# The turned S5 scan: where the swapped operand is written, and where copies, lengths, samples and Toeplitz loads stand

## The chip, the core and the metric

The kernel runs on one core of a Trainium2 chip. The metric is the device time of one execution in microseconds, the median of several runs. TensorE (PE in the profile) does the matrix products, VectorE (DVE), ScalarE (ACT) and GpSimd (POOL) work on tiles, and transfers are issued from the queues of SyncE (SP) and of GpSimd.

## The reference, cut to what matters

The reference is one step of a two-layer decoder: layer 0 mixes tokens with an HGRN2 gated recurrence, layer 1 with an S5 complex diagonal recurrence; each layer has a SwiGLU channel mixer and a per-layer embedding ("ple"). There are 512 prompt tokens and 8 samples of 8 tokens, D = 1024. The change lies in the S5 mixer of layer 1:

```
bu = einsum('btgc,gpc->btgp', u, b_bar);  bu[:, 0] += lam_bar * h0
h  = associative_scan(s5_combine, (lam_bar, bu))       # h_t = lam_bar * h_(t-1) + bu_t, complex
y  = einsum('btgp,gcp->btgc', h, c_mat).real + d * u;  y = gelu(y)
val, gate = split(y @ w_glu);  out = val * sigmoid(gate);  new states: h[:, -1]
```

It has 64 groups of 16 channels with 64 complex states each. The samples start from h0, the prompt from zero.

## The kernel before

**Accuracy.** Products are taken in three parts (`mm3`, L299 to L301): the weight and the activation are each split into a high and a low part (whi, wlo; xh, xl), and whi·xh, whi·xl and wlo·xh are added in one PSUM bank. A weight tile is loaded to `wraw`, copied by ScalarE to `whi` (L200, `copy`), and subtracted on another engine to `wlo` (L203, `tt`); in the S5 stage that engine is GpSimd, and GpSimd's queue issues the loads of `wraw` (L226). There are four PSUM banks named `mm`.

**Chunks.** S5 is computed in chunks of 8 tokens, 36 to a block, in two blocks of 288 columns. Block 0 holds the first KA = 28 chunks of the prompt and the 8 samples (one chunk each), block 1 the prompt's other 36. `z_part(blk, o, ...)` multiplies octet o (8 groups) of the tokens `u` by the input matrices `zw` (L1447). ScalarE copies the result out of PSUM: the chunks' inputs go to `HS[blk]` (tiles "xl", 128 x 64 x 36; partitions 0 to 63 real, 64 to 127 imaginary), the last ones to `ZL`.

**The turned scan.** The recurrence over chunks is complex. The kernel turns every input backward by a rotation that depends on group and chunk, scans with real factors, and turns the result forward. The rotation tables are `C` (name "turn") and `Z` (name "xh"), which are loaded from `tb_scratch` (L1577). A quarter is 16 groups. In `turn`, two multiplies of 64 partitions each make the cross term with halves exchanged (into `pr`, L203), a third multiplies by C, and a fourth adds or subtracts. `run_on` does the scan (L1533) with the factors `rho` spread over 35 columns, and then `lengths` copies the next quarter's factors into the single buffer (L1529). All of this is on VectorE.

**The order in `layer0_to_1`.** It runs under a manual schedule: each engine's instructions stand in the order in which the program writes them, and an engine works through them strictly in that order.

1. While the ple of layer 0 ends (`tails`, `pj` and `xf` rows at L203 and L206), the queue of SP issues two octets of the Toeplitz matrices `mg` (L1453), then the two tables.
2. For block 0, octet by octet, `z_part(0, o)`, with the ple tail of block 1 in between (`start(1, ...)`, `settle(1)`). Then VectorE scans the four quarters of block 0.
3. SP stores the layer's result (`u_scratch`) and loads it as `u` in 16 pieces. TensorE computes the projection of layer 1's embedding (`ple_proj`), which ScalarE copies to `pj1`.
4. GpSimd's queue loads the samples' state h0 into a tile `sm` (L1618). ScalarE scales it into HS[0] in place of the samples' columns, behind the block-0 scan (L197). Then `z_part(1, o)`.
5. `lag_part` (Toeplitz products within a chunk) and `out_part` (products of the states, added to u by VectorE, gelu by ScalarE, stored to `y_scratch`, loaded back by `y_load`), with the block-1 scan (`last_states`) on VectorE in steps between them.
6. `last_samples` advances the samples by their last chunk, on GpSimd (SE = 1) at the first lag, scales on ScalarE and stores (L1632, `out_s5s`).
7. `y_load` splits the loaded y into XH (ScalarE) and XL; for block 0 all eight XL splits are on GpSimd. XL[0] uses the memory of HS[0] once that is no longer read. Then come the GLU products, four banks at first, and the sigmoid (`gs`).

Of the kernel before, what the change touches and what calls it, by code (L numbers as in the profile page):

```python
# [8 lines left out]
FP32 = mybir.dt.float32  # L9
# [3 lines left out]
ACT = mybir.ActivationFunctionType  # L13
OP = mybir.AluOpType
# [18 lines left out]
KA = 28  # L33
# [32 lines left out]
SCAN_AT = ((2, 4, 10, 16, 20, 26, 30, 34, 38, 42, 46, 50, 54, 60, 68, 74), (2, 4, 6, 9, 12, 15, 17, 19, 21, 23, 26, 33, 34, 36, 41, 45))  # L66
QWAIT = 9
SIDE = 1
OCT = 2
TB = 3  # L70
SL = (0, 0, 1, 0, 1, 0, 1, 0)
SO0 = (0, 1, 0, 1, 0, 1, 0, 1)
SE = 1
SO = 0
SF = 3
YD = 4
WX = 3
AB = 2
# [64 lines left out]
def hybrid_decoder_kernel(ctx: ExitStack, tc: tile.TileContext, a: dict):  # L143
    nc = tc.nc
# [37 lines left out]
    SGN, NSG = sgn[:, 0:1], sgn[:, 1:2]  # L182
# [13 lines left out]
    def act(out, in_, func, bias=None, scale=1.0):  # L196
        nc.scalar.activation(out, in_, func, bias=ZERO if bias is None else bias, scale=scale)  # L197

    def copy(out, in_):
        nc.scalar.activation(out, in_, ACT.Copy)  # L200

    def tt(out, x, y, op, eng=None):
        (eng or nc.vector).tensor_tensor(out, x, y, op=op)  # L203
# [137 lines left out]
    def settle(blk):  # L341

        while any(it[1] == blk for it in later):
            it = next(it for it in later if it[1] == blk)
            later.remove(it)
            it[2]()
        if blk in tails:
            run(tails.pop(blk))
# [10 lines left out]
    def step(g, n=1):  # L359
        for _ in range(n):  # L360
            if next(g, StopIteration) is StopIteration:
                return False
        return True
# [11 lines left out]
    class LayerNorm:  # L375
# [747 lines left out]
    mg_d = nc.dram_tensor("mg_scratch", (128, NG, 128), FP32).ap()  # L1123
# [287 lines left out]
    U, HS = {}, {}  # L1411
# [11 lines left out]
    def step_rows(scratch):  # L1423
        return scratch.rearrange("s c g k -> (s c) (g k)")
# [10 lines left out]
    def u_load(m, blk):  # L1435
        nc.sync.dma_start(U[blk][:, 8 * m:8 * m + 8, :].rearrange("p g k -> p (g k)"), step_rows(u_d[blk, m]))

    def products(w, o, x):

        ps = mm_bank()
        xo = x[:, 8 * o:8 * o + 8, :].rearrange("p g k -> p (g k)")
        for j in range(8):
            c = slice(36 * j, min(36 * j + SW, NB))
            for r in (0, 64):
                nc.tensor.matmul(ps[r:r + 64, c], w[:, j, r:r + 64], xo[:, c], start=True, stop=True)  # L1447
                passed(0.2)
        return ps[:, :NB].rearrange("p (g k) -> p g k", k=36)

    def octet(pool, src, o, tag, bufs, eng=None):
        t = pool.tile([128, 8, 128], FP32, tag=tag, name=tag, bufs=bufs)
        (eng or nc.sync).dma_start(t, src[:, 8 * o:8 * o + 8, :])  # L1453
        return t

    def z_part(blk, o, zw):

        v = products(zw, o, U[blk])
        g = slice(8 * o, 8 * o + 8)
# [38 lines left out]
    def chunk_state(j):  # L1498
        return HS[0][:, :, j] if j < KA else HS[1][:, :, j - KA]

    def advance(out, hj, z, n=None, work=None, lam=lam8, gs=slice(0, NG), eng=None):

        ng = gs.stop - gs.start

        def b(t):
            return t[:, gs] if n is None else t[:, gs, None].to_broadcast([128, ng, n])
        sh = [128, NG] if n is None else [128, NG, n]
        m, c = work or [const.tile(sh, FP32, tag=t, name=t, bufs=AB) for t in ("am", "ac")]
        lrb, lib = b(lam[:, 0]), b(lam[:, 1])
        tt(m, hj, lrb, OP.mult, eng)  # L1510
        tt(c[0:64], hj[64:128], lib[64:128], OP.mult, eng)
        tt(c[64:128], hj[0:64], lib[0:64], OP.mult, eng)
        tt(m, m, z, OP.add, eng)
        tt(out, m, c, OP.add, eng)

    def turn(blk, q, back):

        gs, n = slice(16 * q, 16 * q + 16), slice(1, 36 if blk else KA + 1)  # L1520
        h, c, C, Z = (x[:, n] if len(x.shape) == 2 else x[:, :, n] for x in
                      (HS[blk][:, gs], s5["c"], s5["C"][:, gs], s5["Z"][:, gs]))
        tt(c[0:64], h[64:128], Z[64:128], OP.mult)
        tt(c[64:128], h[0:64], Z[0:64], OP.mult)
        tt(h, h, C, OP.mult)
        tt(h, h, c, OP.add if back else OP.subtract)

    def lengths(q):
        nc.vector.tensor_copy(s5["rho"][:, :, 1:36], rho[:, 16 * q:16 * q + 16, None].to_broadcast([128, 16, 35]))  # L1529

    def run_on(blk, q):
        h = HS[blk][:, 16 * q:16 * q + 16].rearrange("p g k -> p (g k)")
        nc.vector.tensor_tensor_scan(h, s5["rho"].rearrange("p g k -> p (g k)"), h, 0.0, op0=OP.mult, op1=OP.add)  # L1533
        lengths((q + 1) % 4)

    s5 = {}

    def layer0_to_1():
# [28 lines left out]
        st.update(lo=nc.gpsimd, split=SPLIT_S5, limit=N_SLOTS)  # L1567
        op_pool = ExitStack()
        op = op_pool.enter_context(tc.tile_pool(name="op", bufs=1, side="right"))
        mg, cl = [octet(op, mg_d, o, "mg", OCT) for o in range(OCT)], []  # L1570

        s5["C"] = op.tile([128, NG, 36], FP32, name="turn")
        turn_z = {}
# [1 line left out]
        s5["Z"] = turn_z[1]  # L1575
        for n, x in enumerate((s5["C"], s5["Z"])):
            nc.sync.dma_start(x.rearrange("p g k -> p (g k)"), tb_d[:, n].rearrange("p g k -> p (g k)"))  # L1577
        s5["rho"], s5["c"] = (x for x in s5["zp"].tile([128, 2, 16, 36], FP32, tag="praw", name="pr2").rearrange(
            "p n g k -> n p g k"))
        settle(0)  # L1580
        for b in range(2):
            chunk_tiles("xl", HS, b)
        nc.vector.memset(HS[0][:, :, 0:1], 0.0)
        nc.vector.memset(s5["rho"][:, :, 0:1], 0.0)
        lengths(0)


        for o in range(8):
            z_part(0, o, s5["zw"][o])
            if o == 1:  # L1590
                start(1, LIGHT)
            elif o > 1:
                step(tails[1], 2)
        settle(1)
        for q in range(4):
            turn(0, q, True)
            run_on(0, q)
            turn(0, q, False)
        nc.vector.tensor_copy(HS[1][:, :, 0], HS[0][:, :, KA])
        left.close()  # L1600
        pj1 = left.enter_context(tc.tile_pool(name="pp1", bufs=1)).tile([128, KD, T], FP32, name="pj1")
# [3 lines left out]
        for b in (1, 0):  # L1605
            U[b] = U["both"][:, b]
            for n in range(KD):
                u_load(n, b)


        def samples(tag, n=1):
            t = s5["zp"].tile([128, n, NG, 8], FP32, tag=tag, name="sm")
            return [t[:, i] for i in range(n)]
# [2 lines left out]
        run(proj)  # L1616
        h0, = samples("phi")
        nc.gpsimd.dma_start(h0, a["h0"])  # L1618
        act(HS[0][:, :, KA:36], h0, ACT.Identity, scale=NSG)
        for o in range(8):  # L1620
            z_part(1, o, s5["zw"][o])
            if len(mg) < 8:
# [3 lines left out]
        so, tmp = samples("plo", 2)  # L1626

        def last_samples():
            advance(so, HS[0][:, :, KA:36], ZL[:, :, 0:8], 8, (so, tmp), eng=SE and nc.gpsimd)
            yield  # L1630
            act(so, so, ACT.Identity, scale=NSG)
            nc.gpsimd.dma_start(a["s5s"], so)  # L1632
            yield

        samples_end = last_samples()
# [3 lines left out]
        def last_states():  # L1639
            for q in range(4):  # L1640
                turn(1, q, True)
                run_on(1, q)
                yield
                turn(1, q, False)
                yield
            advance(po, chunk_state(63), ZL[:, :, 8])
            nc.vector.tensor_scalar(po, po, NSG, None, op0=OP.mult)
            nc.gpsimd.dma_start(a["s5o"], po)
            yield
# [5 lines left out]
        def y_start(b, o):  # L1655

            if o > 1:
                y_loads[b, o - 2] = y_load(b, o - 2, yt[b][o - 2])
                step(y_loads[b, o - 2])

        yt = [[U[0][:, 8 * o:8 * o + 8].rearrange("p g k -> p (g k)") for o in range(8)]] * 2
        for o in range(8):
            lag_part(o, mg[o])
            if o >= OCT:
                cl.append(octet(s5["zq"], cl_d, len(cl), "zw", 8))
            step(scan, SL[o])
            if o == SO:
                step(samples_end)
        for o in range(8):
            out_part(0, o, cl[o])  # L1670
            y_start(0, o)
            step(scan, SO0[o])
            if o >= YD:
                step(y_loads[0, o - YD])
            if o == SF:
                step(samples_end)
        y_start(0, 8)
        y_start(0, 9)
        for o in range(8 - YD, 8):
# [8 lines left out]
        with more_weights(WX, (p0 + 128) // 8):  # L1688
            for blk, m in [(b, m) for h in (0, 4) for b in range(2) for m in range(h, h + 4)]:
                p = p0 + 16 * m  # L1690
# [205 lines left out]
```

## Time and profile before

| | |
|---|---|
| median of 3 runs | 1588.85 us (1588.47 to 1592.74) |
| the profiled execution | 1589.6 us |
| its span | 1587.8 us |
| mean granted TensorE clock | 0.983 |
| busy: PE, DVE, ACT, POOL | 95%, 60%, 43%, 22% of the span |
| the S5 stage with the change | about 896 to 994 us |

Times in the views are microseconds from the start of the span. A row of a timeline gives start, duration, engine, line, operation, output and inputs with their shapes, and in brackets the idle time ahead of it and what ended that. A row of the waits gives who waited for what: total, number, longest. A row of the groups gives the count, the busy time and mean nanoseconds of one, and the idle time before.

### The profile page before, as it was taken

Reading aid. Unit: us, or ns where it says so; the run is one execution under the profiler, and the core shown is the slowest. Engines: PE = TensorE matmul, PEld = TensorE weight load, DVE = VectorE, ACT = ScalarE, POOL = GpSimd, SP = SyncE. Lnnn points to the kernel's source line nnn. Section 1 sums busy time; section 2 is a strip of 40 time slices with the busy share of each in tenths; the row PEclk is TensorE's granted clock in tenths of the full one; section 3 lists DMA queues with packets and bytes.
Section 4 is the critical chain, followed back from the end, with each engine's and each line's share of the span. In section 5 each row is a group of like instructions: output and inputs, shape, how many; then the busy total and the mean of one; then the engine's idle time right before and its main releaser. Section 6 shows DMA issues by size and latency. Waiting matters only on the chain. (4 is left out here: it accounts for less than half of the span.)

```text
span 1587.8 us, 30040 instructions
## 1 busy us (share of the span) xinstructions
PE 1514.9 (95%) x12550; PEld 1467.1 (92%) x12550; DVE 947.1 (60%) x1711; ACT 687.9 (43%) x1152; POOL 342.9 (22%) x447
## 2 busy tenths in 40 slices
PE   8899999899999999999999947999999999999998
PEld 7898989788999999999989947899999999999997
DVE  4848484868547778953486699457433233334685
ACT  5546464746532223123278524436432222123375
POOL 1303030302003768860022332302000000000111
PEclk9999999999999999999999978999999999999999
DMA  5223131232224877663214986432222222223121
GB/s 185 95 69 101 63 109 64 100 115 80 68 70 145 216 185 216 195 182 108 98 54 170 233 209 179 101 107 80 67 80 93 80 81 93 81 80 120 31 78 60
DMA packets 97255, 180.32 MB, mean 114 GB/s; under 512 B 41888, under 2 KB 56912, under 8 KB 96864
## 3 DMA queue, kind: packets, MB, share of 16 engines
q1 hardware_dynamic: 88144, 151.92, 31.3%
q0 software_dynamic: 8976, 26.49, 6.2%
q8 instruction: 98, 1.61, 0.4%
q14 instruction: 37, 0.30, 0.1%
HBM read 151.08 MB, written 27.30 MB: 112 GB/s over the span
## 5 line engine op out<-in xcount | busy, mean ns | idle before, releaser
L299 PE MATMUL mm<-xh,whi 128*128 128x288 f32 x2048 | 609.7, 298 | 9.5 <-ACT xh L200 6.5
L300 PE MATMUL mm<-xl,whi 128*128 128x288 f32 x2048 | 608.9, 297 | 5.0 <-POOL xl L203 3.5
L301 PE MATMUL mm<-xh,wlo 128*128 128x288 f32 x2048 | 606.6, 296 | 1.3 <-DVE wlo L203 1.3
L299 PEld LDWEIGHTS mm<-xh,whi 128*128 128x128 f32 x2048 | 387.8, 189 | 15.9 <-ACT xh L200 7.6
L300 PEld LDWEIGHTS mm<-xl,whi 128*128 128x128 f32 x2048 | 387.9, 189 | 8.4 <-POOL xl L203 5.0
L301 PEld LDWEIGHTS mm<-xh,wlo 128*128 128x128 f32 x2048 | 387.8, 189 | 1.5 <-DVE wlo L203 1.5
L200 ACT ACTIVATE whi<-wraw 128x1024 fp32r<-128x1024 f32 x208 | 218.7, 1053 | 250.1 <-DMA wraw<-in_w_dram 117.2
L203 DVE TENSOR_TENSOR wlo<-wraw,whi 128x1024 fp32r<-128x1024 f32 x200 | 247.1, 1252 | 33.2 <-ACT whi L200 32.8
L299 PE MATMUL mm<-hhi,whi 128*128 128x288 f32 x704 | 209.3, 297 | 0.0
L301 PE MATMUL mm<-hhi,wlo 128*128 128x288 f32 x704 | 207.5, 295 | 0.0
L300 PE MATMUL mm<-hlo,whi 128*128 128x288 f32 x704 | 207.2, 294 | 0.0
L203 DVE TENSOR_TENSOR fs<-fs,mm 128x288 f32<-128x288 f32 x88 | 39.9, 454 | 254.5 <-PE mm L301 241.4
L203 POOL TENSOR_TENSOR ln_s<-ln_s,xf 128x288 f32<-128x288 f32 x24 | 24.3, 1012 | 570.9 <-DVE xf L203 451.2
L299 PEld LDWEIGHTS mm<-hhi,whi 128*128 128x128 f32 x704 | 132.1, 188 | 1.7 <-issue 1.4
L300 PEld LDWEIGHTS mm<-hlo,whi 128*128 128x128 f32 x704 | 132.1, 188 | 0.3
L301 PEld LDWEIGHTS mm<-hhi,wlo 128*128 128x128 f32 x704 | 132.0, 188 | 0.0
L299 PE MATMUL mm<-xhi,whi 128*128 128x320 f32 (+1 forms) x384 | 121.5, 316 | 0.0
L300 PE MATMUL mm<-xlo,whi 128*128 128x320 f32 (+1 forms) x384 | 113.3, 295 | 0.0
L301 PE MATMUL mm<-xhi,wlo 128*128 128x320 f32 (+1 forms) x384 | 113.2, 295 | 0.0
L200 ACT ACTIVATE hhi<-fs 128x288 fp32r<-128x288 f32 x88 | 38.8, 441 | 152.1 <-DVE fs L203 152.1
L197 ACT ACTIVATE fs<-mm,eps 128x288 f32<-128x288 f32 x88 | 44.1, 502 | 131.0 <-PE mm L301 130.9
L299 PEld LDWEIGHTS mm<-xhi,whi 128*128 128x128 f32 x384 | 72.7, 189 | 6.9 <-issue 4.4
(318 smaller groups left out, 2273.9 us busy)
## 6 DMA issues: line engine op xcount, KB each, us to landing
wraw<-in_w_dram SPq DMA_DIRECT2D x198, 512.0 KB
wraw<-in_w_dram POOLq DMA_DIRECT2D x10, 512.0 KB, 7.1
S<-in_s_dram SPq DMA_DIRECT2D x8, 512.0 KB
out_hgs_dram<-So SPq DMA_DIRECT2D x8, 512.0 KB
wr<-wt_scratch SPq DMA_DIRECT2D x16, 256.0 KB
bT<-in_s5bt_dram SPq DMA_DIRECT2D x16, 256.0 KB
cl_scratch<-cl POOLq DMA_DIRECT2D x16, 256.0 KB, 6.1
zw_scratch<-zw POOLq DMA_DIRECT2D x16, 256.0 KB, 6.5
```

The lines of the kernel that those rows point to most:

```text
L197: nc.scalar.activation(out, in_, func, bias=ZERO if bias is None else bias, scale=scale)
L200: nc.scalar.activation(out, in_, ACT.Copy)
L203: (eng or nc.vector).tensor_tensor(out, x, y, op=op)
L299: nc.tensor.matmul(out, whi, rhi, start=start, stop=False)
L300: nc.tensor.matmul(out, whi, rlo, start=False, stop=False)
L301: nc.tensor.matmul(out, wlo, rhi, start=False, stop=stop)
```

## The change

1. `z_part(0, o)`: ScalarE writes each octet's prompt inputs twice more, half by half with the halves exchanged, into a tile `swap` (one for a quarter, two buffers). The backward turn of block 0 then multiplies that tile by Z in one instruction of 128 partitions, in place of two of 64, and subtracts in place of adding.
2. `lengths` goes from VectorE to GpSimd and has two buffers: two copies at the start, and six more, each of which waits for a scan.
3. Quarter 0 of block 0 is scanned inside the loop over `z_part(0, o)`, ahead of block 1's ple tail; quarters 1 to 3 follow that tail.
4. The loads of `mg` are issued after the 16 loads of u, not before the tables; one goes to a tile of its own (OCT = 1), seven to used `zw` tiles.
5. h0 is scaled on VectorE.
6. The samples' advance is on VectorE, after the whole block-1 scan.

The core of the diff:

```diff
-OCT = 2
+OCT = 1
...
         if blk == 0:
             copy(HS[0][:, g, 1:36], v[:, :, 0:35])
+            q, i = divmod(o, 2)
+            if i == 0:
+                swapped[q] = s5["op"].tile([128, 16, 36], FP32, tag="swap", name="swap", bufs=2)
+            x = swapped[q][:, 8 * i:8 * i + 8, 1:KA + 1]
+            copy(x[0:64], v[64:128, :, 0:KA])
+            copy(x[64:128], v[0:64, :, 0:KA])
             copy(ZL[:, g, 0:8], v[:, :, KA:36])
...
-        tt(c[0:64], h[64:128], Z[64:128], OP.mult)
-        tt(c[64:128], h[0:64], Z[0:64], OP.mult)
+        if back and not blk:
+            tt(c, c, Z, OP.mult)
+        else:
+            tt(c[0:64], h[64:128], Z[64:128], OP.mult)
+            tt(c[64:128], h[0:64], Z[0:64], OP.mult)
         tt(h, h, C, OP.mult)
-        tt(h, h, c, OP.add if back else OP.subtract)
+        tt(h, h, c, OP.add if back and blk else OP.subtract)
...
-        nc.vector.tensor_copy(s5["rho"][:, :, 1:36], rho[:, 16 * q:16 * q + 16, None].to_broadcast([128, 16, 35]))
+        nc.gpsimd.tensor_copy(s5["rho"][q % 2][:, :, 1:36],
+                              rho[:, 16 * q:16 * q + 16, None].to_broadcast([128, 16, 35]))
...
-        lengths((q + 1) % 4)
+        if (blk, q) < (1, 2):
+            lengths((q + 2) % 4)
+
+    def scan_quarter(blk, q):
+        turn(blk, q, True)
+        run_on(blk, q)
+        turn(blk, q, False)
...
-        mg, cl = [octet(op, mg_d, o, "mg", OCT) for o in range(OCT)], []
...
             if o == 1:
                 start(1, LIGHT)
+                scan_quarter(0, 0)
             elif o > 1:
                 step(tails[1], 2)
         settle(1)
-        for q in range(4):
-            turn(0, q, True)
-            run_on(0, q)
-            turn(0, q, False)
+        for q in range(1, 4):
+            scan_quarter(0, q)
...
                 u_load(n, b)
+        mg, cl = [octet(op, mg_d, o, "mg", OCT) for o in range(OCT)], []
...
-        act(HS[0][:, :, KA:36], h0, ACT.Identity, scale=NSG)
+        nc.vector.tensor_scalar(HS[0][:, :, KA:36], h0, NSG, None, op0=OP.mult)
...
-            advance(so, HS[0][:, :, KA:36], ZL[:, :, 0:8], 8, (so, tmp), eng=SE and nc.gpsimd)
+            advance(so, HS[0][:, :, KA:36], ZL[:, :, 0:8], 8, (so, tmp))
...
+            step(samples_end, 2)
             advance(po, chunk_state(63), ZL[:, :, 8])
...
             step(scan, SL[o])
-            if o == SO:
-                step(samples_end)
```

In the changed file the lines up to about 1450 stand three lower (L203 becomes L200, L200 becomes L197, L226 becomes L223); L1529 becomes L1539, L1533 L1544, L1618 L1637.

On GpSimd, from block 1's `xf` additions to the load of h0 (`sm`), before:

```order
L203 TENSOR_TENSOR xf<-xf,pj 128x288 [waits DVE_49] x4
L203 TENSOR_TENSOR wlo<-wraw,whi 128x1024 [waits DMASW1_49,PE_49,Activation_49]
L226 DMA wraw<-in_w_dram 128x1024 [waits DMASW3_49,Pool_49]
L203 TENSOR_TENSOR wlo<-wraw,whi 128x1024 [waits DMASW2_49,PE_49,Activation_49]
L226 DMA wraw<-in_w_dram 128x1024 [waits DMASW4_49,Pool_49]
L1618 DMA sm<-in_h_dram 128x512 [waits DMASW5_49,PE_49]
```

and after:

```order
L1539 COPY pr_10102<-rho 128x16x35 [waits DVE_49]
L200 TENSOR_TENSOR xf<-xf,pj 128x288 [waits DVE_49] x4
L200 TENSOR_TENSOR wlo<-wraw,whi 128x1024 [waits DMASW1_49,PE_49,Activation_49]
L223 DMA wraw<-in_w_dram 128x1024 [waits DMASW3_49,Pool_49]
L1539 COPY pr_10102<-rho 128x16x35 [waits DVE_49] x3
L200 TENSOR_TENSOR wlo<-wraw,whi 128x1024 [waits DMASW2_49,PE_49,Activation_49]
L223 DMA wraw<-in_w_dram 128x1024 [waits DMASW4_49,Pool_49]
L1637 DMA sm<-in_h_dram 128x512 [waits DMASW5_49,PE_49]
```

Four copies of the lengths stand among these rows now (`pr`; each waits for a scan on VectorE: the first for block 0's quarter 0, the others for its quarters 1, 2 and 3), and the load of h0 stands behind all four.

On VectorE, the end of the block-1 scan (`xl1` is HS[1], `xl0` HS[0], `am` and `ac` the prompt's last state), before:

```order
L1533 SCALAR_TENSOR_TENSOR xl1_10108<-pr2_10106,xl1_10108 128x576 [waits DVE_49]
L1529 COPY pr2_10106<-rho_87 128x16x35 [waits DVE_49]
L203 TENSOR_TENSOR pr2_10106<-xl1_10108,xh1_10103 64x16x35 x2
L203 TENSOR_TENSOR xl1_10108<-xl1_10108,turn_10102 128x16x35 [waits DVE_49]
L203 TENSOR_TENSOR xl1_10108<-xl1_10108,pr2_10106 128x16x35 [waits DVE_49]
L203 TENSOR_TENSOR am_11097<-xl1_10108,lam8_86 128x64 [waits DVE_49]
```

and after:

```order
L1544 SCALAR_TENSOR_TENSOR xl1_10104<-pr2_10102,xl1_10104 128x576 [waits DVE_49,Pool_49]
L200 TENSOR_TENSOR swap_11088<-xl1_10104,xh1_10099 64x16x35 [waits DVE_49]
L200 TENSOR_TENSOR swap_11088<-xl1_10104,xh1_10099 64x16x35
L200 TENSOR_TENSOR xl1_10104<-xl1_10104,turn_10098 128x16x35 [waits DVE_49]
L200 TENSOR_TENSOR xl1_10104<-xl1_10104,swap_11088 128x16x35 [waits DVE_49]
L200 TENSOR_TENSOR sm_10703<-xl0_10103,lam8_86 128x512
L200 TENSOR_TENSOR sm_10703<-xl0_10103,lam8_86 64x512 x2
L200 TENSOR_TENSOR sm_10703<-sm_10703,zl_88 128x512 [waits DVE_49]
L200 TENSOR_TENSOR sm_10703<-sm_10703 128x512 [waits DVE_49]
```

The scan (SCALAR_TENSOR_TENSOR in these rows) now waits for GpSimd, the copy of the lengths is gone from here, and the samples' advance (`sm`) stands behind the last quarter; its first three instructions are the last that read HS[0].

On ScalarE, the copies out of PSUM for octets 4 to 6 of block 0, after:

```order
L197 ACTIVATE xl0_10103<-mm_10242 128x8x35 [waits PE_49]
L197 ACTIVATE swap_10263<-mm_10242 64x8x28 [waits DVE_49]
L197 ACTIVATE swap_10263<-mm_10242 64x8x28
L197 ACTIVATE zl_88<-mm_10242 128x8x8
L197 ACTIVATE xl0_10103<-mm_10267 128x8x35 [waits PE_49]
L197 ACTIVATE swap_10263<-mm_10267 64x8x28 x2
L197 ACTIVATE zl_88<-mm_10267 128x8x8
L197 ACTIVATE xl0_10103<-mm_10288 128x8x35 [waits PE_49]
L197 ACTIVATE swap_10309<-mm_10288 64x8x28 [waits DVE_49,Activation_49]
```

and the same octets before:

```order
L200 ACTIVATE xl0_10107<-mm_10225 128x8x35 [waits PE_49]
L200 ACTIVATE zl_88<-mm_10225 128x8x8
L200 ACTIVATE xl0_10107<-mm_10247 128x8x35 [waits PE_49]
L200 ACTIVATE zl_88<-mm_10247 128x8x8
L200 ACTIVATE xl0_10107<-mm_10266 128x8x35 [waits PE_49]
L200 ACTIVATE zl_88<-mm_10266 128x8x8
```

Two instructions to an octet are added; the first one that writes a reused `swap` tile waits for VectorE.

More of the change, by code (lines that the diff above doesn't have):

```diff
@@ L72 @@
 SO0 = (0, 1, 0, 1, 0, 1, 0, 1)
-SE = 1
-SO = 0
-SF = 3
 YD = 4
@@ L1514, in advance @@
         tt(out, m, c, OP.add, eng)
+    swapped = {}
     def turn(blk, q, back):
         gs, n = slice(16 * q, 16 * q + 16), slice(1, 36 if blk else KA + 1)
-        h, c, C, Z = (x[:, n] if len(x.shape) == 2 else x[:, :, n] for x in
-                      (HS[blk][:, gs], s5["c"], s5["C"][:, gs], s5["Z"][:, gs]))
-        tt(c[0:64], h[64:128], Z[64:128], OP.mult)
-        tt(c[64:128], h[0:64], Z[0:64], OP.mult)
+        if blk and back:
+            swapped[q] = s5["op"].tile([128, 16, 36], FP32, tag="swap", name="swap", bufs=2)
+        h, c, C, Z = (t[:, :, n] for t in (HS[blk][:, gs], swapped[q], s5["C"][:, gs], s5["Z"][:, gs]))
+        if back and not blk:
[3 more added lines that the diff above has]
+            tt(c[64:128], h[0:64], Z[0:64], OP.mult)
         tt(h, h, C, OP.mult)
-        tt(h, h, c, OP.add if back else OP.subtract)
+        tt(h, h, c, OP.add if back and blk else OP.subtract)
     def lengths(q):
-        nc.vector.tensor_copy(s5["rho"][:, :, 1:36], rho[:, 16 * q:16 * q + 16, None].to_broadcast([128, 16, 35]))
+        nc.gpsimd.tensor_copy(s5["rho"][q % 2][:, :, 1:36],
+                              rho[:, 16 * q:16 * q + 16, None].to_broadcast([128, 16, 35]))
     def run_on(blk, q):
         h = HS[blk][:, 16 * q:16 * q + 16].rearrange("p g k -> p (g k)")
-        nc.vector.tensor_tensor_scan(h, s5["rho"].rearrange("p g k -> p (g k)"), h, 0.0, op0=OP.mult, op1=OP.add)
-        lengths((q + 1) % 4)
+        nc.vector.tensor_tensor_scan(h, s5["rho"][q % 2].rearrange("p g k -> p (g k)"), h, 0.0,
+                                     op0=OP.mult, op1=OP.add)
+        if (blk, q) < (1, 2):
[4 more added lines that the diff above has]
+        turn(blk, q, False)
     s5 = {}
@@ L1569, in layer0_to_1 @@
         op = op_pool.enter_context(tc.tile_pool(name="op", bufs=1, side="right"))
-        mg, cl = [octet(op, mg_d, o, "mg", OCT) for o in range(OCT)], []
+        s5["op"] = op
         s5["C"] = op.tile([128, NG, 36], FP32, name="turn")
@@ L1577, in layer0_to_1 @@
             nc.sync.dma_start(x.rearrange("p g k -> p (g k)"), tb_d[:, n].rearrange("p g k -> p (g k)"))
-        s5["rho"], s5["c"] = (x for x in s5["zp"].tile([128, 2, 16, 36], FP32, tag="praw", name="pr2").rearrange(
-            "p n g k -> n p g k"))
+        s5["rho"] = [x for x in s5["zp"].tile([128, 2, 16, 36], FP32, tag="praw", name="pr2").rearrange(
+            "p n g k -> n p g k")]
         settle(0)
@@ L1583, in layer0_to_1 @@
         nc.vector.memset(HS[0][:, :, 0:1], 0.0)
-        nc.vector.memset(s5["rho"][:, :, 0:1], 0.0)
-        lengths(0)
+        for q in range(2):
+            nc.gpsimd.memset(s5["rho"][q][:, :, 0:1], 0.0)
+            lengths(q)
         for o in range(8):
@@ L1674, in layer0_to_1 @@
                 step(y_loads[0, o - YD])
-            if o == SF:
-                step(samples_end)
         y_start(0, 8)
```

## The prediction

> **What bounds the kernel now.** I read the page's busy shares first, then the waits between 896 and 996 us, then the timelines of ScalarE, TensorE, VectorE (DVE) and GpSimd (POOL) there. Before that stretch the change touches nothing; what it is worth is how much earlier or later TensorE gets its work inside it.
>
> ```profile
> PE 1514.9 (95%) x12550; PEld 1467.1 (92%) x12550; DVE 947.1 (60%) x1711; ACT 687.9 (43%) x1152; POOL 342.9 (22%) x447
> ```
>
> TensorE is idle for 73 of 1587.8 us. The two longest waits of the S5 stage:
>
> ```profile
> PE mm L1447 <- ACT zl L200: 12.1, 1, 12.1
> ...
> PE mm L1447 <- DMA u<-u_scratch: 8.2, 1, 8.2
> ```
>
> ScalarE's and TensorE's rows say who holds whom:
>
> ```profile
> 908.30 1.32 ACT L200 ACTIVATE pj<-mm 128x288 f32<-128x288 f32 x4 [3.75 <-POOL xf L203]
> ...
> 918.97 0.69 ACT L200 ACTIVATE pj<-mm 128x288 f32<-128x288 f32 x2
> 943.53 0.81 ACT L197 ACTIVATE xl<-sm,eps,sgn 128x512 f32<-128x512 f32 x1 [23.87 <-DVE xl L1599]
> ...
> 990.45 2.01 ACT L200 ACTIVATE whi<-wraw 128x1024 fp32r<-128x1024 f32 x2 [3.11 <-DVE xl L203]
> ```
>
> ```profile
> 926.75 5.94 PE L1447 MATMUL mm<-u,zw 128*64 128x64 f32 x128 [8.19 <-DMA u<-u_scratch]
> ...
> 979.11 0.61 PE L299 MATMUL mm<-xh,whi 128*128 128x288 f32 x1 [1.43 <-DVE u L203]
> ...
> 992.50 0.29 PE L301 MATMUL mm<-xh,wlo 128*128 128x288 f32 x1
> ...
> 994.32 0.40 PE L299 MATMUL mm<-xh,whi 128*128 128x288 f32 x1 [1.52 <-ACT gs L197]
> ```
>
> ScalarE's scaling of h0 at 943.53 stands behind DVE's whole block-0 scan, and TensorE behind ScalarE. Then DVE's block-1 scan runs; the first GLU units start at 979.11, last until 992.79 (13.7 us), and TensorE goes on at 994.32, 3.87 us after ScalarE's whi copies began at 990.45. So DVE bounds the stage, and 979.11 and 994.32 are the marks that matter: from there TensorE has work, and a shift of the second mark goes to the end.
>
> **The change, step by step.** All times are on the clock of before. DVE's rows of block 0:
>
> ```profile
> 900.45 0.52 DVE L206 SCALAR_TENSOR_TENSOR pj<-pj,vec,pr 128x288 f32<-128x288 f32 x1 [4.36 <-ACT pr L197]
> ...
> 909.65 2.08 DVE L203 TENSOR_TENSOR pr<-xl,xh 64x448 f32<-64x448 f32 x2 [2.25 <-DMA xh<-tb_scratch]
> ...
> 913.15 3.43 DVE L1533 TENSOR_TENSOR_SCAN xl<-pr,xl 128x576 f32<-128x576 f32 x1
> ...
> 928.88 1.25 DVE L203 TENSOR_TENSOR pr<-xl,xh 64x448 f32<-64x448 f32 x2
> 930.16 0.63 DVE L203 TENSOR_TENSOR xl<-xl,turn 128x448 f32<-128x448 f32 x1
> ...
> 931.49 1.36 DVE L1533 TENSOR_TENSOR_SCAN xl<-pr,xl 128x576 f32<-128x576 f32 x1
> 932.88 0.45 DVE L1529 COPY pr<-rho 128x560 f32<-128x560 f32 x1
> ...
> 935.30 0.63 DVE L203 TENSOR_TENSOR xl<-xl,pr 128x448 f32<-128x448 f32 x1
> ```
>
> and POOL's, which run beside them:
>
> ```profile
> 907.48 0.79 POOL L203 TENSOR_TENSOR xf<-xf,pj 128x288 f32<-128x288 f32 x1 [0.83 <-DVE pj L206]
> 908.23 2.39 POOL L203 TENSOR_TENSOR wlo<-wraw,whi 128x1024 fp32r<-128x1024 f32 x1
> ...
> 912.90 2.46 POOL L203 TENSOR_TENSOR wlo<-wraw,whi 128x1024 fp32r<-128x1024 f32 x1 [1.42 <-ACT whi L200]
> ...
> 918.86 0.54 POOL L1618 DMA_DIRECT2D sm<-in_h_dram  x1 [2.64 <-PE mm L301]
> ...
> 944.43 4.11 POOL L203 TENSOR_TENSOR sm<-xl,lam 128x512 f32<-128x512 f32 x3 [21.72 <-ACT xl L197]
> ...
> 972.75 0.55 POOL L1632 DMA_DIRECT2D out_s5s_dram<-sm  x1 [16.55 <-issue]
> ...
> 987.41 0.80 POOL L203 TENSOR_TENSOR xl<-u,xh 128x288 fp32r<-128x288 f32 x1 [0.49 <-ACT xh L200]
> ```
>
> A scan alone takes 1.36 us, and 3.43 us while a wlo of 2.46 us runs on POOL: DVE stands still for about as long as POOL's instruction lasts. I therefore charge every POOL instruction that falls beside DVE's scans with its full length. The Trainium skill, "SBUF — State Buffer", section "Who interferes with whom", says that a DVE instruction with two SBUF inputs contends with a GpSimd instruction that reads SBUF. The 3.43 us here agree; by it the moved copies, which read rho, would hold DVE as well, and that speaks against this change.
>
> (1) Swapped copies. In block 0 the backward turn's two half multiplies (1.25) become one full one (0.63): -0.62 a quarter on DVE. The 16 new ScalarE copies are hidden at first behind DVE's wait for its tables. Their cover goes for octets 4 and 6: those reuse a swap tile, and wait for quarter 0 and for quarter 1's forward turn. Behind octet 6 stand ScalarE's copies of the ple projection, the four PSUM banks and TensorE.
>
> (2) Lengths on POOL: -0.45 on DVE a quarter. A quarter of block 0 goes from 7.05 us (928.88 to 935.93) to 7.05 - 0.62 - 0.45 = 6.0; I use 6.05 with gaps. On POOL no copy of 128x560 was timed; the nearest rows:
>
> ```profile
> L1238 POOL TENSOR_SCALAR tZ<-tZ,sgn 128x1152 f32<-128x1152 f32 x2 | 6.4, 3216 | 0.1
> ...
> L492 POOL MEMSET att<- 128x512 f32 x2 | 1.0, 524 | 0.0
> ```
>
> Lower bound 0.52 (a fill, with no input), upper 3216 x 560/1152 = 1.56; I take the middle, 1.0. Six copies follow a scan each, so each lies beside the next DVE work: +6.0 (bounds 3.1 to 9.4). The Trainium skill, "GPSIMD Engine Reference", section 4.1 "Engine selection", has one-input work on GpSimd roughly at line rate; an estimate from it and DVE's 0.45 for the same copy is 0.6 us, 2.4 us less over the six, and the end at 1598.
>
> (3) Toeplitz loads behind the u loads. What goes out from ahead of the tables:
>
> ```profile
> core 0: us, PE busy (x) PEld busy (x) DVE busy (x) ACT busy (x) POOL busy (x), PEclk, DMA share, GB/s
> 896.00:900.00 4.00, 4.00 (x118) 3.57 (x115) 0.10 (x1) 3.78 (x10) 2.92 (x2) 1.00 0.98 315
> ```
>
> ```profile
> mg<-mg_scratch SPq DMA_DIRECT2D x2, 512.0 KB
> ...
> sm<-in_h_dram POOLq DMA_DIRECT2D x1, 256.0 KB, 7.5
> out_s5s_dram<-sm POOLq DMA_DIRECT2D x1, 256.0 KB, 2.3
> ```
>
> 1.05 MB at 315 GB/s are 3.3 us; I take 3, so tables at 906.6 instead of 909.65 (bounds 903, twice that, and no gain). The loads' new place, behind 16 u loads on SP, costs nothing: the lag products come after block 1's products, which are late anyway.
>
> (4) Quarter 0 ahead of block 1's tail: 906.6 + 6.05 + one copy 1.0 = 913.65. The tail's rows (900.45 to 907.48 before, 7.0 us) now end at 920.6, 13.2 later, and with them the u loads: TensorE's first block-1 product moves from 926.75 to about 940.
>
> (5) Quarter 1: 920.6 + 6.05 + wlo 2.4 + last xf add 0.8 + copy 1.0 = 930.85. ScalarE is held until here; the projection's copies (908.30 to 919.66 before, 11.4) bring TensorE to about 943. Quarter 2 ends at 930.85 + 7.05 = 937.9, quarter 3's scan 3.4 later, at 941.3.
>
> (6) h0. On POOL its DMA issue stands behind the last of the three copies, a wlo and a weight load: 941.3 + 1.0 + 2.4 + 0.9 (0.54 for an issue and what I allow between instructions) = 945.6 (before: 918.86). Landing took 7.5 us for this load and 2.3 for a store of the same size; I take 4.8, the middle: 950.5. h0's scaling, now on DVE ahead of the block-1 scan, about 0.5: block 1 starts at 951.0, where before:
>
> ```profile
> 945.02 2.60 DVE L203 TENSOR_TENSOR pr<-xl,xh 64x560 f32<-64x560 f32 x2 [1.58 <-ACT xl L200]
> ...
> 958.78 1.49 DVE L203 TENSOR_TENSOR pr<-xl,xh 64x560 f32<-64x560 f32 x2
> ...
> 961.86 1.36 DVE L1533 TENSOR_TENSOR_SCAN xl<-pr,xl 128x576 f32<-128x576 f32 x1
> ...
> 965.19 1.48 DVE L203 TENSOR_TENSOR pr<-xl,xh 64x560 f32<-64x560 f32 x2
> ...
> 968.15 0.81 DVE L203 TENSOR_TENSOR u<-u,mm 128x288 f32<-128x288 f32 x2
> ...
> 989.62 0.74 DVE L203 TENSOR_TENSOR xl<-xl,pr 128x560 f32<-128x560 f32 x1
> ```
>
> (7) Block 1. A clean quarter is 4.44 (958.78 to 963.22) and a forward turn of 1.48 + 2 x 0.74 = 3.0: 7.5. Four, eight u adds at 0.41, one wlo and two copies: 30 + 3.3 + 2.4 + 2.0 = 37.8, so 988.8 (before 945.02 to 990.36, 45.3, with the samples' advance, 4.11 us and more, and the XL splits of POOL beside it).
>
> (8) The samples' advance, moved from POOL at 944.43 to DVE behind the whole scan. It reads HS[0], whose memory XL[0] reuses; POOL's eight XL[0] splits, the last of them at 987.41 before, must wait for its first three instructions: 3 x 0.69 (0.74 x 512/560) = 2.1, then a split, 0.8. TensorE's GLU units can start at 991.8 instead of 979.11: **+12.7**. They last 13.7, to 1005.5. ScalarE's way there is as long: eight splits of 0.8 to 0.9 to about 998.2, the samples' store 0.55 + 2.3 to 1001, whi and on 3.87 to 1005. TensorE goes on at about 1006 instead of 994.32.
>
> Sum: +11.7 us on this execution of 1589.6 us (span 1587.8 and 1.8 outside it), which lies 0.75 above the median of 1588.85: forecast 1600.5.
>
> **Rivals.** *Faster.* POOL's reads don't hold DVE up: then 1.0 in quarter 0, 4.2 in quarter 1, 1.0 in quarter 2 and 4.4 in block 1 go, the scan ends at 978.2 and TensorE starts at 981: 1590. With the tables at 903 and h0 after 2.3 us (6.1 together) it starts at 975, its units end 5.6 us ahead of 994.32, and the time is about 1583. It decides when TensorE starts before 975.8, so that the units end 4.8 us ahead. For it: DVE loses 4 x 1.07 us of work in block 0, and the advance's 4.11 us on POOL no longer lie beside block 1. Against: 3.43 beside 1.36.
>
> *Within 0.3%* (4.8 us, about what a measurement of this kernel can tell from no change). Copies at 0.52 (-2.9), h0 after 2.3 us (-2.5), tables another 2 us earlier: +11.7 - 7.4 = +4.3, about 1593.
>
> *The loads' move doesn't do what it says.* If tables wait for something other than the Toeplitz loads, 909.65 stays (+3), and with copies of 1.56 (+3.4) and h0 after 7.5 (+2.7): +20.8, about 1609.
>
> **How the numbers follow.** The forecast, +5 to +16, has 0.58; the last rival 0.14; within 0.3% 0.18; faster 0.10, since step 8 makes DVE's end TensorE's start and only a scan 13 us earlier pays that back. The range cuts 0.1 at each side: 1588 to 1608 (the forecast's own: 1594 to 1605). Slower by over 0.3% is 0.58 + 0.14 = 0.72.
>
> **What would show it.** Right: TensorE waiting, ahead of its first GLU units, for POOL's xl, and POOL for DVE's sm; DVE waiting for the h0 load ahead of block 1; ScalarE's swap copies waiting for DVE; scans over 2 us beside POOL's copies; whi waiting for the samples' store. Wrong: the block-1 scan ending before 975, POOL copies of 0.5 us or scans of 1.36 us beside them, h0 issued before 940.

## The result, and the profile after

The changed kernel takes 1599.51 us (median of 6 runs, 1594.33 to 1600.91), the kernel before 1590.12 us in its 6 runs: a ratio of 1.0055, 95% interval 1.0037 to 1.0074. The forecast was 1600.5, slower, within 1588 to 1608. The profiled execution of after took 1600.91 us, with a span of 1599.1 us.

The two traces have no common zero in this stage. The first input product of block 0 on TensorE (first row before, second after) serves as the mark:

```profile
895.01 2.06 PE L1447 MATMUL mm<-xh,zw 128*64 128x64 f32 x64 [1.01 <-DMA xh<-u_scratch]
```

```profile
892.98 2.06 PE L1444 MATMUL mm<-xh,zw 128*64 128x64 f32 x64 [0.90 <-DMA xh<-u_scratch]
```

So 2.0 us are added to a time of after to compare it with one of before. The waits of after between 896 and 1010 us (who waits for what: total, number, longest):

```profile
POOL xl L200 <- DVE sm L200: 26.0, 1, 26.0
...
ACT swap L197 <- DVE xl L200: 21.3, 2, 13.1
...
PE mm L297 <- POOL xl L200: 13.9, 1, 13.9
...
ACT whi L197 <- DMA out_s5s_dram<-sm: 7.8, 1, 7.8
DVE xl L1638 <- DMA sm<-in_h_dram: 6.0, 1, 6.0
...
DVE u L200 <- PE mm L1444: 3.1, 2, 2.0
```

This is a chain that the waits of before do not have. VectorE's advance of the samples (sm) holds GpSimd's XL splits, these hold TensorE for 13.9 us, and the store of the samples holds ScalarE's whi copies. The last of these holds cost TensorE nothing here: ScalarE's next activation (gs, at 1004.63) waited 1.32 us for TensorE. Their places in time, on VectorE, GpSimd, ScalarE and TensorE:

```profile
986.69 0.74 DVE L200 TENSOR_TENSOR xl<-xl,swap 128x560 f32<-128x560 f32 x1
987.35 2.10 DVE L200 TENSOR_TENSOR sm<-xl,lam 128x512 f32<-128x512 f32 x3
```

```profile
989.67 6.97 POOL L200 TENSOR_TENSOR xl<-u,xh 128x288 fp32r<-128x288 f32 x8 [25.97 <-DVE sm L200]
```

```profile
1000.00 2.01 ACT L197 ACTIVATE whi<-wraw 128x1024 fp32r<-128x1024 f32 x2 [7.79 <-DMA out_s5s_dram<-sm]
...
1004.63 0.50 ACT L194 ACTIVATE gs<-mm,eps 128x288 f32<-128x288 f32 x1 [1.32 <-PE mm L298]
```

```profile
976.62 0.40 PE L296 MATMUL mm<-xh,whi 128*128 128x288 f32 x1 [3.29 <-ACT xh L197]
...
990.87 0.61 PE L297 MATMUL mm<-xl,whi 128*128 128x288 f32 x1 [13.86 <-POOL xl L200]
...
1005.23 0.36 PE L296 MATMUL mm<-xh,whi 128*128 128x288 f32 x1
```

Before, the same two matmuls, the first of the GLU units and the first that needs XL, stood at:

```profile
975.22 0.40 PE L299 MATMUL mm<-xh,whi 128*128 128x288 f32 x1 [3.48 <-ACT xh L200]
976.11 0.61 PE L300 MATMUL mm<-xl,whi 128*128 128x288 f32 x1 [0.49 <-POOL xl L203]
```

In after, TensorE does one GLU matmul at 976.62 and stops at the first that needs XL. The block-1 scan ends at 987.43, the advance's first three instructions at 989.45, and the first split begins 0.2 us later. The first use of XL is 16.8 us later than before on one clock (990.87 + 2.0 against 976.11). Not all of that is lost, because TensorE's work before was broken by waits and in after it is not. TensorE goes on behind the first GLU units at 1005.23, or 1007.2 on before's clock, where before had 994.32: 12.9 us later.

### The profile page after: what moved, and what is told of

The parts are those of the page before. It is cut to its first block, busy times and chain, and to the rows that moved or that the text cites. A ratio compares the mean times of both kernels' runs of the same rounds, so it can differ in the third digit from the quotient of the medians.

```text
span 1599.1 us, 30060 instructions
## 1 busy us (share of the span) xinstructions
PE 1511.3 (95%) x12550; PEld 1463.7 (92%) x12550; DVE 940.2 (59%) x1703; ACT 694.4 (43%) x1167; POOL 342.1 (21%) x452
## 3 DMA queue, kind: packets, MB, share of 16 engines
q8 instruction: 98, 1.61, 0.4%
## 4 chain that ended last, share of the span: by engine, by line
PE 76%; DVE 13%; ACT 5%; DMA 3%; issue 2%; POOL 1%; SPq 0%; DVEq 0%; POOLq 0%; ACTq 0%
PE mm L296 24%; PE mm L297 23%; PE mm L298 23%; DVE b L577 1%; DVE wlo L200 1%; DVE xf L200 1%; DVE xl L200 1%; PE mm L1444 1%; ACT whi L197 1%; PE tr L706 1%; DMA xh<-tb_scratch 1%; DVE K L200 1%; DVE ln_q L200 1%; DVE swap L200 1%; DVE ln_z L200 1%
## 5 line engine op out<-in xcount | busy, mean ns | idle before, releaser
L297 PE MATMUL mm<-xl,whi 128*128 128x288 f32 x2048 | 609.0, 297 | 18.5 <-POOL xl L200 16.8
L197 ACT ACTIVATE whi<-wraw 128x1024 fp32r<-128x1024 f32 x208 | 218.6, 1053 | 243.9 <-DMA wraw<-in_w_dram 121.6
L200 DVE TENSOR_TENSOR wlo<-wraw,whi 128x1024 fp32r<-128x1024 f32 x200 | 246.9, 1251 | 28.5 <-ACT whi L197 28.0
L200 DVE TENSOR_TENSOR fs<-fs,mm 128x288 f32<-128x288 f32 x88 | 39.9, 454 | 254.8 <-PE mm L298 241.7
L200 POOL TENSOR_TENSOR ln_s<-ln_s,xf 128x288 f32<-128x288 f32 x24 | 24.3, 1011 | 571.1 <-DVE xf L200 451.1
L197 ACT ACTIVATE hhi<-fs 128x288 fp32r<-128x288 f32 x88 | 38.9, 441 | 151.7 <-DVE fs L200 151.7
```

The lines of the kernel that those rows point to most:

```text
L297: nc.tensor.matmul(out, whi, rlo, start=False, stop=False)
```

## Experiments

Each ratio is to the kernel before, run on the same chip with it; its medians there lay between 1589.3 and 1589.7 us.

**Where the loss is: e1 to e4.** The advance comes first.

```diff
# e1, against after: advance on GpSimd at the first lag, as before
+            advance(so, ..., (so, tmp), eng=nc.gpsimd)
+            if o == 0: step(samples_end)          # in the lag loop; scale and store at out_part 3
-            step(samples_end, 2)                  # behind the scan
```

> The changed kernel with only the samples' advance put back: on GpSimd at the first lag product, scale and store later, as before. Theory (the advance, behind the whole block-1 scan, holds the XL[0] splits and so TensorE's GLU units): the splits start near 976 us as before, TensorE no longer waits 13.9 us for them, the block-1 scan is stretched by up to 4 us by GpSimd's advance and ends near 991, and the time falls by about 9 us to 1590 (1588 to 1593). Rival (block 0 is at fault: quarter 0 ahead of the ple tail, and h0 late behind GpSimd's copies, delay everything behind them): the time stays at 1597 or more.

Measured: 1588.87 us, ratio 1.0000 (0.9991 to 1.0009). The whole loss is gone with one edit. The last quarter of its scan shows what it pays in return, VectorE and GpSimd side by side:

```profile
982.90 1.77 DVE L1544 TENSOR_TENSOR_SCAN xl<-pr,xl 128x576 f32<-128x576 f32 x1
984.71 2.43 DVE L200 TENSOR_TENSOR swap<-xl,xh 64x560 f32<-64x560 f32 x2
```

```profile
984.28 3.53 POOL L200 TENSOR_TENSOR xl<-u,xh 128x288 fp32r<-128x288 f32 x3 [0.81 <-ACT xh L197]
```

With the splits free early, they lie beside the scan's end and stretch it (2.43 for a pair that takes 1.49 alone).

```diff
# e2, against before: only the advance moved behind the block-1 scan, on VectorE
-            advance(so, ..., eng=SE and nc.gpsimd)
+            advance(so, ...)
+            step(samples_end, 2)                  # in last_states, behind the scan
```

> The kernel before with only the samples' advance moved to VectorE behind the whole block-1 scan. Theory: the scan ends some 4 us earlier, near 986, since GpSimd's advance no longer lies beside it, but the XL[0] splits start only near 988, TensorE's GLU units near 989 instead of 979, and the time rises by 8 to 10 us to about 1598. Rival (block 0 is at fault): no more than 2 us above before, and by the shorter scan rather below it.

Measured: 1595.01 us, 1.0036 (1.0023 to 1.0050): +5.7, the sign of the theory and below its 8 to 10. TensorE's row shows the same stop:

```profile
986.28 0.61 PE L300 MATMUL mm<-xl,whi 128*128 128x288 f32 x1 [14.06 <-POOL xl L203]
```

This trace's first input product stands at 892.4, 2.6 before that of the kernel before; on before's clock 986.28 is 988.9, and the forecast was 989. From the first input product to the matmul with which TensorE goes on behind the first GLU units, before takes 99.3 us, e2 108.5, after 112.2 and e1 100.2. So e2 loses 9.2 us in the stage, as forecast, and after 12.9, and the ratios show some 4 us less of both (5.7 and 8.7).

For after the traces give part of the reason. VectorE gets its tables 12.3 us behind the first input product there, and 9.6 to 10.5 us behind it in e1, e3, e5, e8, e10 and e11, which load them at the same point. So about 2 of the 12.9 us belong to the profiled execution and not to the change. For e2 it is not settled. Executions of one kernel lie up to 9 us apart (before, beside e13: 1585.58 to 1594.91).

```diff
# e3, against after: advance still on VectorE, between the lag products and out_part
+            if o == 7: step(samples_end)          # in the lag loop
-            step(samples_end, 2)
```

> The changed kernel with the samples' advance still on VectorE, but ahead of the first out_part, where VectorE is idle for 3 us waiting for TensorE. Theory: nothing holds the XL[0] splits, the scan ends within 1 us of where it does now, ScalarE's whi copies follow it directly, and the time is about 1587.5 (1585 to 1590), below e1 by what GpSimd's advance costs VectorE. Rival (block 0 is at fault): 1596 or more.

Measured: 1590.17 us, 1.0003 (0.9994 to 1.0011). The hold is gone, but e3 isn't below e1: on VectorE the advance costs about what GpSimd's costs beside it, and the splits, which now lie beside the last part of the scan, cost VectorE 3.8 us there, which the expectation left out. The advance is still on VectorE here, so the loss of after comes from its place and not from its engine.

```diff
# e4, against after: quarter 0 behind block 1's ple tail, as before
-                scan_quarter(0, 0)                # in the z loop
+        for q in range(4): scan_quarter(0, q)     # behind settle(1)
```

> The changed kernel with quarter 0 of block 0 scanned behind block 1's ple tail, as before. Theory: the tail fills VectorE's wait for the tables again, so block 0's scan ends about 6 us earlier, the u loads come 13 us earlier, the block-1 scan starts 5 us earlier, and since the end is the scan's end plus the advance, the time falls by about 5 us to 1594.5. Rival (the place of quarter 0 alone is the whole loss): falls by 10 us to 1590. Rival (it is hidden): no change, 1599.

Measured: 1598.29 us, 1.0053 (1.0040 to 1.0065), no difference from after that can be told. The expectation failed: two other waits took the place of the one taken away. TensorE's row:

```profile
920.79 0.61 PE L296 MATMUL mm<-phi,whi 128*128 128x288 f32 x1 [13.51 <-ACT zl L197]
```

ScalarE, waiting to reuse a swap tile, held the projection, and the load of h0 behind it was issued at 941.19, although block 0's last scan had ended at 935.26. That is 46.0 us behind this trace's first input product, as in e3 (46.1), where quarter 0 comes first. Then VectorE waited 4.9 us for TensorE at the first u additions, 3.1 in after.

**What the other parts are worth: e5, e6, e7, e11.**

```diff
# e5, against e3: four swap tiles; OCT = 0 makes room
-OCT = 1
+OCT = 0
-  swapped[q] = s5["op"].tile([128, 16, 36], ..., bufs=2)      # both places
+  swapped[q] = s5["op"].tile([128, 16, 36], ..., bufs=4)
```

> e3 with four swap tiles in place of two (their memory is that of the one Toeplitz tile, whose load goes to a used zw tile), so that ScalarE no longer waits for quarters 0 and 1. Theory (the block-1 scan's start is set by VectorE's and GpSimd's order: the tail behind quarter 0, h0 behind the copies of the lengths): TensorE's 12.4 us wait goes, but h0 is still issued near 942 and the u loads still come after the tail, so block 1 starts at most 2 us earlier: 1588.5 (1587 to 1590). Rival (ScalarE's hold by the swap tiles is a loss of the change in full): 10 us less than e3, 1580.

Measured: 1594.31 us, 1.0036 (1.0024 to 1.0049): neither, 4 us slower than e3. With ScalarE's wait gone it was slower. GpSimd's, SP's and VectorE's rows of e5:

```profile
941.24 0.54 POOL L1637 DMA_DIRECT2D sm<-in_h_dram  x1
```

```profile
935.79 5.65 SPq L1450 DMA_DIRECT2D zw<-mg_scratch  x8
941.83 17.33 SPq L1450 DMA_DIRECT2D zw<-cl_scratch  x8
```

```profile
950.70 2.22 DVE L1638 TENSOR_SCALAR xl<-sm,sgn 128x512 f32<-128x512 f32 x1 [6.46 <-DMA sm<-in_h_dram]
```

h0 was issued earlier than in after (46.4 us behind the first input product, 49.1 in after) and lands 9.4 us after its issue instead of 5.6. The earlier TensorE frees the zw tiles, so SP's Toeplitz and output loads (mg and cl) go out ahead of it and beside it: in the 5 us ahead of its issue the DMA engines are busy for a share of 0.95 in e5 and 0.58 in after. That these loads make it late is argued and not tested; in e6 they go out ahead of it as well, and it lands after 6.0 us. e11 tests whether the late h0 is the loss.

```diff
# e11, against e5: h0 scaled only ahead of the advance
-        nc.vector.tensor_scalar(HS[0][:, :, KA:36], h0, NSG, None, op0=OP.mult)   # ahead of z_part(1)
+            (the same line, first in last_samples)
```

> e5 with VectorE's scaling of h0 moved from ahead of the block-1 scan to just ahead of the samples' advance, so that a late h0 holds up nothing. Theory (e5 was 4 us slower than e3 because h0 landed 9.5 us after its issue, beside 16 loads that SP had issued early): the block-1 scan starts near 945 and not 952.9, VectorE then waits for TensorE for a few us at the first u additions, and the time falls by 4 to 6 us to about 1589. Rival (the four swap tiles, or the missing tile of its own for the first Toeplitz octet, cost by themselves, by a later lag product): stays at 1594.

Measured: 1586.93 us, 0.9982 (0.9972 to 0.9993), 7 us below e5. With h0 off VectorE's way, the first scan of block 1 starts 52.7 us behind the trace's first input product, 61.2 in e5. So a late h0 was e5's loss, and the four tiles cost nothing by themselves.

```diff
# e6, against e5: quarter 0 behind the tail (e4's edit)
```

> e5 with quarter 0 behind block 1's ple tail. Theory: in e4 ScalarE's hold hid what the earlier tail gives; with four swap tiles the four quarters run from about 905 to 932, the u loads come 13 us earlier, h0 is issued near 935 and lands near 940, block 1 starts 7 to 8 us earlier than in e3, the scan ends near 984, and the time is about 1581 (1578 to 1584). Rival (quarter 0's place costs nothing, as e4 read alone): within 2 us of e5.

Measured: 1588.16 us, 0.9989 (0.9979 to 0.9998): outside the 1578 to 1584 expected. The step from e5 is 6 us, near the 7 to 8 forecast, from a start that was 6 higher than the forecast took. The same edit was worth nothing in e4: there ScalarE's hold hid it. VectorE still waited 3.05 us for h0:

```profile
942.93 0.49 DVE L1637 TENSOR_SCALAR xl<-sm,sgn 128x512 f32<-128x512 f32 x1 [3.05 <-DMA sm<-in_h_dram]
```

```diff
# e7, against e6: block 0's scans are written behind the issue of h0's load
         h0, = samples("phi")
         nc.gpsimd.dma_start(h0, a["h0"])
+        for q in range(4): scan_quarter(0, q)
```

> e6 with the load of h0 and the projection's weights ahead of block 0's copies of the lengths on GpSimd. Theory: h0 is there before block 0's scan ends, block 1 follows it at once near 934, and the scan ends some 6 us earlier than in e6: about 1576 (1572 to 1580). Rival (TensorE's block-1 products and lag products, which wait for u and the Toeplitz loads, set VectorE's pace by then): within 2 us of e6.

Measured: 1585.22 us, 0.9972 (0.9962 to 0.9983), 3 us below e6: half the step expected, and outside 1572 to 1580. GpSimd issues h0 at 924.87 and VectorE never waits for it:

```profile
947.65 0.48 DVE L1637 TENSOR_SCALAR xl<-sm,sgn 128x512 f32<-128x512 f32 x1
```

VectorE now works without a wait from the tail to the scan's end.

**The parts by themselves: e8, e10, e13.**

```diff
# e8, against e3: the copies of the lengths on VectorE, two buffers kept
-        nc.gpsimd.tensor_copy(s5["rho"][q % 2]...
+        nc.vector.tensor_copy(s5["rho"][q % 2]...
```

> e3 with the copies of the lengths on VectorE (two buffers kept). By the prediction's price (each GpSimd copy holds VectorE for its whole length, 1.0, now measured 1.1) six copies of 0.45 in place of six of 1.1 give back 3.9 us, and h0 is issued 1.1 earlier: about 1586. Rival (the trace of the changed kernel: the pair of half multiplies beside a copy takes 1.61 in place of 1.25, so a copy holds VectorE for 0.36 only): 6 x (0.45 - 0.36), half a microsecond slower at most, no difference that can be measured.

Measured: 1589.44 us, 1.0004 (0.9995 to 1.0012), e3's time. The rival holds, and the prediction's price of the copies falls. e8 also shows that a VectorE copy is held by GpSimd as its two-input work is:

```profile
906.08 0.45 DVE L1539 COPY pr<-rho 128x560 f32<-128x560 f32 x1
...
934.22 2.47 DVE L1539 COPY pr<-rho 128x560 f32<-128x560 f32 x1
```

The second lies beside a wlo (on GpSimd at 933.31, 3.07 us).

```diff
# e10, against e3: no swapped copies; two half multiplies in block 0's backward turn
-            copy(x[0:64], v[64:128, :, 0:KA])
-            copy(x[64:128], v[0:64, :, 0:KA])
```

> e3 without the swapped copies: ScalarE writes the chunks' inputs once, and block 0's backward turn has its two half multiplies back. Theory: VectorE pays 0.62 in each of four quarters, 2.5 us, ScalarE's hold of TensorE goes but was hidden, and the time is 2.5 us above e3: 1592.5 (1591 to 1594). Rival (as in e5 a TensorE that is earlier sets off the Toeplitz loads beside h0's load, which then lands 9.5 us after its issue in place of 5.7): 4 us more, 1596. Second rival (ScalarE's hold cost as much as the multiplies saved): the same as e3, 1590.

Measured: 1594.39 us, 1.0035 (1.0022 to 1.0049): 4.2 us above e3, between theory and first rival. Its scans of block 0 are 7.03 us apart (923.96 to 930.99) and e3's 6.16, so four quarters take 3.5 us more; the multiplies' own time is 0.64 of the 0.87 a quarter (1.26 in place of 0.62). And h0, issued at 944.09, is used only at 952.92. Beside e3's other parts, then, the swapped copies are a gain; the run does not separate what the multiplies and the later h0 give to it.

```diff
# e13, against before: the two Toeplitz octets are loaded behind the u loads
-        mg, cl = [octet(op, mg_d, o, "mg", OCT) for o in range(OCT)], []     # ahead of the tables
+        (the same line, behind the u loads)
```

> The kernel before with only the loads of its two Toeplitz octets moved behind the u loads (the loads' step of the prediction alone). Theory (1.05 MB less ahead of the tables): the tables land about 3 us earlier after their issue, VectorE's idle 2.25 us between the tail and block 0's scan go, the scan ends 2 us earlier, and the time falls by about 2 us to 1587.5; the lag products wait no longer than before, since block 1's products are late. Rival (tables wait for something else): VectorE still waits 2 us, 1589.5. Second rival (the first Toeplitz octet now lands after block 1's products): 2 us or more slower.

Measured: 1587.70 us, 0.9983 (0.9970 to 0.9996), the 2 us of the theory. VectorE goes from the tail into the scan without a wait:

```profile
905.89 0.50 DVE L206 SCALAR_TENSOR_TENSOR pj<-pj,vec,pr 128x288 f32<-128x288 f32 x1
906.43 1.75 DVE L203 TENSOR_TENSOR pr<-xl,xh 64x448 f32<-64x448 f32 x2
```

**A version that beats both: e9.**

```diff
# e9, against e7: swapped copies for block 1 too
+        k = 35 if blk else KA
+        copy(x[0:64], v[64:128, :, 0:k])          # for both blocks
+        copy(x[64:128], v[0:64, :, 0:k])
-        if back and not blk:
+        if back:
             tt(c, c, Z, OP.mult)
```

> e7 with ScalarE writing block 1's inputs with halves exchanged too, so that block 1's backward turn multiplies once, by 128 partitions, as block 0's does. Theory (VectorE is the bound from the tail to the end of the block-1 scan): four times 1.49 - 0.74 = 0.75 less on VectorE, 3 us, and about 1582. Rival (ScalarE's 16 further copies of 0.36, which stand between TensorE's block-1 products and the lag products, and the swap tiles' reuse, make the u additions late, and VectorE waits for TensorE): within 1 us of e7 or slower.

Measured: 1581.96 us, 0.9948 (0.9934 to 0.9962): 3.3 us below e7, as the theory has it. A row of block 1's backward turn:

```profile
951.38 0.74 DVE L200 TENSOR_TENSOR swap<-swap,xh 128x560 f32<-128x560 f32 x1
```

It stands where e7 has a pair of 1.49 us (0.75 less, four times, is 3.0). So after's idea pays once its cost is paid elsewhere: e9 is after with the advance moved, four swap tiles, h0 ahead of the copies, the tail first and the swapped copies for block 1 as well, and lies about 17 us below after (0.9948 and 1.0055 of before).

## Why the prediction was right, point by point

Times of after plus 2.0 us stand against the steps:

| step | forecast | measured |
|---|---|---|
| (3) tables are there | 906.6 | 907.3 |
| (4) quarter 0 ends; tail ends | 913.65; 920.6 | 913.5; 920.4 |
| (5) ScalarE is let go by quarter 1 | 930.85 | 929.2 |
| (6) h0 issued; landed | 945.6; 950.5 | 944.1; 949.8 |
| (7) block 1 starts; its scan ends | 951.0; 988.8 | 950.4; 989.4 |
| (8) first split used by TensorE; TensorE goes on | 991.8; 1006 | 992.9; 1007.2 |

The rows agree to 1.7 us, and part of that is luck. About 2 us of every measured time come from the late tables of this execution. e3 has the same instructions up to the first quarters of block 1; there, on before's clock, the tables are there at 904.6 and block 1 starts at 948.0, 2 to 3 us ahead of the forecast:

```profile
905.44 0.63 DVE L200 TENSOR_TENSOR swap<-swap,xh 128x448 f32<-128x448 f32 x1 [8.21 <-DMA xh<-tb_scratch]
```

(Its first input product stands at 895.81, 0.8 behind that of before.) So the steps up to block 1 were priced somewhat too high. The rows of after that carry the table, and that were not shown above:

```profile
905.25 0.63 DVE L200 TENSOR_TENSOR swap<-swap,xh 128x448 f32<-128x448 f32 x1 [11.08 <-DMA xh<-tb_scratch]
...
908.58 1.61 DVE L200 TENSOR_TENSOR swap<-xl,xh 64x448 f32<-64x448 f32 x2
...
920.05 2.65 DVE L200 TENSOR_TENSOR xl<-xl,swap 128x448 f32<-128x448 f32 x1
...
947.83 0.49 DVE L1638 TENSOR_SCALAR xl<-sm,sgn 128x512 f32<-128x512 f32 x1 [5.97 <-DMA sm<-in_h_dram]
948.35 1.49 DVE L200 TENSOR_TENSOR swap<-xl,xh 64x560 f32<-64x560 f32 x2
```

```profile
908.61 1.10 POOL L1539 COPY pr<-rho 128x560 f32<-128x560 f32 x1 [10.66 <-DVE xl L1544]
...
919.49 2.72 POOL L200 TENSOR_TENSOR wlo<-wraw,whi 128x1024 fp32r<-128x1024 f32 x1
...
942.09 0.54 POOL L1637 DMA_DIRECT2D sm<-in_h_dram  x1 [0.84 <-PE mm L298]
...
963.04 0.66 POOL L1539 COPY pr<-rho 128x560 f32<-128x560 f32 x1 [6.72 <-DVE xl L1544]
```

**Step 8 was right, and it is most of the loss.** e1 and e3 take it away and are at the time of before; e2 puts it alone into before and is slower by 5.7. The other parts of the change, with the advance out of the way, come to nothing together (e3, 1.0003). What they add when the advance is late stays open: after is at 1.0055 and e2 at 1.0036, and the two intervals overlap. Two readings in this step were off. The GLU units before did not start at 979.11 but at 975.22; only the work without a break starts at 979.11. From the first use of XL to the matmul behind the units after takes 14.4 us, where the step has 13.7 for the units. And ScalarE's way, which the step has as equally long, did not count, since ScalarE waited for TensorE at 1004.63.

**Step 2 was mis-sized.** A copy on GpSimd takes 1.10 us, near the 1.0 assumed, but holds VectorE by 0.36 only (1.61 in place of 1.25 for the pair beside it), not by its length. It starts 0.03 us behind the pair's first multiply, which takes its usual 0.62; the second takes 0.98, and the copy itself 0.44 more than alone. While VectorE was idle, one copy took 0.66 (at 963.04). That is near the estimate of 0.6 from the Trainium skill, "GPSIMD Engine Reference", section 4.1, nearer than the middle that I took. Six copies cost about 2 us and not 6. A wlo holds VectorE nearly as priced: 2.0 us (2.65 in place of 0.63), priced at 2.4. The Trainium skill, "SBUF — State Buffer", section "Who interferes with whom", calls the contention an exclusive lock in which the order of issue decides who waits; the trace agrees for the wlo. For the copy too it shows a wait on both sides, so that VectorE loses only what is left of the copy when its second multiply is due.

**Step 7 was right in its sum by two errors.** The copies were priced too high, and a wait was left out: VectorE waits 3.1 us for TensorE ahead of the first two u additions, since u, the Toeplitz loads and so the lag products are late as well (that is read from their order; the profile names no releaser for TensorE's idle time among the lag products). Block 1 took 39.1 us instead of 37.8. That the two errors nearly cancel is luck.

**Steps 1, 4 and 5: costs that cover each other.** ScalarE's hold, the place of quarter 0 and h0's place behind the copies are three waits side by side. To take one away gives nothing (e4) or a loss (e5); together they give 5 us (e3 to e7). The prediction summed along one path, which was right for this kernel, but it did not say for any of these waits which others it hid.

**The rivals.** "Faster" needed GLU work with XL before 975.8; it began at 992.9. That the loads' move does nothing is refuted by e13. Within 0.3% would have needed copies at 0.52, and by their hold they came below that; but the tables came 0.7 later than forecast in this execution (1 to 2 us earlier than forecast in e1, e3, e5, e8, e10 and e11), h0 was there only after 5.7 us, and the wait for TensorE came on top.

**The signs.** One sign named for a right forecast did not show, and could not have: scans over 2 us beside GpSimd's copies. All eight scans of after take 1.36 us. Each of the six copies waits for a scan to end, so it lies beside what follows the scan and not beside the scan.

## What to carry to other kernels

When work is moved to a place where its engine is free, look first at whose memory it reads: a read that moves behind a scan holds every tile that takes over that memory, on engines that the change doesn't mention. Two or three waits that end at about the same time must be removed together; one alone reads as worthless or harmful, and an engine that is let go earlier may start transfers that delay a later one. A good part of a change can be hidden by a bad one, so time the parts apart before dropping the whole.

## What the runs showed of the hardware

- A GpSimd copy of 128x560 that reads a repeated factor takes 0.66 us alone and 1.10 us beside VectorE's two-input work, and VectorE loses 0.36 us. A wlo of 128x1024 takes 2.4 us alone and 2.7 in after when it begins while such work runs on VectorE, and VectorE loses 2.0 us (at 919.49).
- VectorE's one-input copy of 128x560 is held as well: 0.45 us alone, 2.47 us beside a wlo. The Trainium skill, "SBUF — State Buffer", section "Who interferes with whom", names copies among the instructions that can contend; this trace agrees.
- One load of 256 KB (h0) landed 5.6 us after its issue in after, and 9.4 us in e5, where SP had just issued eight loads of 512 KB to the zw tiles. It took 6.0 us in e6, where such loads went out ahead of it too, so these loads alone do not give the time.
